# One plain tile pair instead of two in the second FFN, and the fourth block's low part by DMA

## The chip, the cores and the metric

The kernel runs on one core of a Trainium2 chip, in one launch. The metric is the time of one execution on the device, in microseconds (us); less is better. The kernel before takes 1185.99 us, the median of three executions from 1185.46 to 1186.32.

Five engines with queues of their own work side by side. TensorE (PE in the profile) multiplies matrices out of on-chip memory into accumulator banks, and loads stationary weights beside that (PEld). VectorE (DVE) and ScalarE (ACT) do elementwise work. GpSimd (POOL) issues the DMAs that add to what they write, and SyncE (SP) issues the ordinary loads.

## The reference

The program is one encoder layer and a final norm: FFN 1, a mixer of two recurrences, FFN 2. Two sequences of 256 tokens go through it. Of it the two FFNs matter here; both have a model width of 1024 and a hidden width of 2816:

```python
def swiglu(h, w_in, w_out):
    a, g = jnp.split(h @ w_in, [D_FF], axis=-1)
    return (jax.nn.silu(a) * g) @ w_out
...
    x = x + 0.5 * swiglu(rmsnorm(x, g_ffn1), w_ffn1_in, w_ffn1_out)
...
    x = x + 0.5 * swiglu(rmsnorm(x, g_ffn2), w_ffn2_in, w_ffn2_out)
```

Everything is float32.

## The kernel before

Both sequences are held together as 512 columns, with features on the 128 partitions, so `x` is eight tiles of 128 x 512. TensorE works in a rounded form of float32, so each operand is split: a high part (a cast to the rounded form) and a low part (value minus high part). A product takes three passes, high by high, high by low and low by high. So each weight tile must be split before it is used. There are two ways. `split2` casts on ScalarE (line 254) and subtracts on VectorE (line 255). `split_dma` casts on ScalarE, writes the negated value into the low tile on ScalarE too, and lets a GpSimd DMA add the weights to it from memory (lines 259 to 261); there VectorE has no part.

An FFN has 22 tile pairs, each a value tile and a gate tile of 128 features. They are computed in three ways:

- The first three pairs (`first_tiles`, tiles `f2i`) run before the norm of x is known, and are scaled by it later in `gated`.
- The next two are plain pairs (`w_plain`, `plain`, tiles `f2p`): 48 matmuls of 512 columns each, on split x. Their value tile's weights come through the tile kind `sum` and the pool `wb`, the gate tile's through `raw` and `wa`.
- The remaining 17 are seven-product units (tiles `f1s`, `f2s`). Value and gate tile by the two halves of the columns is a 2 x 2 block product, which is done with seven products instead of eight, on sums of the weights' four blocks and on sums of x. Each product is 12 matmuls of 256 columns, so a unit is 84.

The sums of x (`x_sums`, lines 310 to 313, tiles `xu`, `xv`, `xt`, `xw`, split into `xch` and `xcl`) are made once in an FFN. The weights of a unit come in two steps. `w_rows` loads them: blocks 1 and 2 into `raw[:, 0:2]`, block 3 into `sm[:, 0]`, block 4 into `raw[:, 2]` (SyncE, lines 335 to 337, "the third load" is that of line 337), and splits blocks 1 and 2 with the accumulating DMA (lines 339 to 341; `wah`, `wal`). `w_sums` forms the weight sums on VectorE (lines 347 to 350), splits three of them (`ah[:, 2:5]`), and then splits the sum in `raw[:, 1]` together with block 4 in `raw[:, 2]` (`wbh`, `wbl`, 1024 elements). Block 4 serves the seventh product, which runs only in the following unit.

`pair` is one unit. On TensorE come product y0 (block 1) and z1 (block 2), the sixth product of the unit before, y4, the seventh of the unit before, q2 and y3. Between them ScalarE copies banks: `m` after y0 (line 419), the right half of `u` after y4 (line 426), which must be done before y3 overwrites that bank, and the left half of `u` after y3 (line 432). VectorE's `t` (line 399) and ScalarE's silu (line 422) come from z1 and m.

The units are grouped in three parts of the hidden tiles (0 to 7, 8 to 14, 15 to 21), and each part is followed by eight output tiles. So the first part has three units, the others seven. `raw`, `sum`, `wa` and `wb` have two buffers each, so the loads of unit n+2 wait until unit n's splits have read theirs. The order of instructions on each engine is set by a scheduler when the program is built, and by a few explicit constraints (`tc.issue_after`); on the chip each queue then runs in that order and waits where its inputs aren't there.

Of the kernel before, what the change touches and what calls it, by code (L numbers as in the profile page):

```python
# [13 lines left out]
ALU = mybir.AluOpType  # L14
# [4 lines left out]
T = 512  # L19
# [17 lines left out]
def encoder_kernel(ctx: ExitStack, tc: tile.TileContext, xT, par, w2, gnorm, mask,  # L37
# [215 lines left out]
    def split2(hi, lo, src):  # L253
        rounded[:] = [nc.scalar.copy(hi, src).ins]
        return nc.vector.tensor_tensor(out=lo, in0=src, in1=hi.bitcast(F32), op=ALU.subtract)
# [76 lines left out]
    def w_rows(w_a, j, name):  # L332

        raw, sm = w_raw(name), w_sum(name)
        nc.sync.dma_start(raw[:, 0:2, :].rearrange("p a b -> p (a b)"), w_a[2 * j])
        nc.sync.dma_start(sm[:, 0, :], w_a[2 * j + 1][:, 0:T])
        nc.sync.dma_start(raw[:, 2, :], w_a[2 * j + 1][:, T:])
        (ah, al), (bh, bl) = w_pair("wa", 5, name), w_pair("wb", 2, name)
        nc.scalar.copy(ah[:, 0:2], raw[:, 0:2])
        nc.scalar.activation(al[:, 0:2], raw[:, 0:2], AF.Copy, scale=-1.0)  # L340
        nc.gpsimd.dma_start(al[:, 0:2].rearrange("p a b -> p (a b)"), w_a[2 * j], accum_op=ALU.add)
        return raw, sm, ah, al, bh, bl

    def w_sums(w_a, j, name, rows=None):

        raw, sm, ah, al, bh, bl = rows or w_rows(w_a, j, name)
        nc.vector.tensor_tensor(out=sm[:, 1], in0=sm[:, 0], in1=raw[:, 2], op=ALU.add)
        nc.vector.tensor_tensor(out=sm[:, 0::2], in0=sm[:, 0:2], in1=raw[:, 0:1].broadcast_to([P, 2, T]),
                                op=ALU.subtract)
        nc.vector.tensor_tensor(out=raw[:, 1], in0=raw[:, 1], in1=sm[:, 2], op=ALU.subtract)  # L350
        split2(ah[:, 2:5], al[:, 2:5], sm)
        split2(bh, bl, raw[:, 1:3])
        a, b = (lambda n: (ah[:, n], al[:, n])), (lambda n: (bh[:, n], bl[:, n]))

        return a(0), a(1), a(2), a(3), a(4), b(0), b(1)
# [37 lines left out]
        split2(hi, lo, raw)  # L393
        return hi, lo

    def ffn(w_a, w_o, xs_of, raws, dma_from, gcol, sq, name, done, last=None, squares={}, places=(None, None), rounds=None):

        L, R = slice(0, SEQ), slice(SEQ, T)
        add = lambda o, p, q: nc.vector.tensor_tensor(out=o, in0=p, in1=q, op=ALU.add)
        late, copied = [], []  # L400
        hs = []
        xc = []

        def finish(late, when):
            j, w, y, q, u, t, g = late
            if when == 0:
                product(y, w[5], xc[X22], False, True)
                nc.scalar.activation(t[:, R], y[:, :SEQ], AF.Silu)
            else:
                product(q, w[6], xc[XT4], False, True)  # L410
                add(g[:, L], q[:, :SEQ], u[:, R])
                hs.append(activate(t, g, f"{name}{j}"))

        def pair(j, w):
            y, z = acc(f"psy_{name}{j}"), acc(f"psz_{name}{j}")
            m, u = tmp(f"{name}m{j}"), tmp(f"{name}u{j}")
            t, g = tmp(f"{name}t{j}"), tmp(f"{name}g{j}")
            product(y, w[0], xc[X11], True, False)
            copied.append(nc.scalar.copy(m[:, L], y[:, :SEQ]).ins)
            product(z, w[1], xc[X21], True, True)  # L420
            add(t[:, L], z[:, :SEQ], m[:, L])
            nc.scalar.activation(t[:, L], t[:, L], AF.Silu)
            if late:
                finish(late[0], 0)
            product(y, w[4], xc[XT2], False, False)
            nc.scalar.copy(u[:, R], y[:, :SEQ])
            if late:
                finish(late.pop(), 1)
            q = acc(f"psq_{name}{j}", True)
            product(q, w[2], xc[XT3], True, False)  # L430
            product(y, w[3], xc[XT1], False, False)
            nc.scalar.copy(u[:, L], y[:, :SEQ])
            add(g[:, R], q[:, :SEQ], u[:, L])
            late.append((j, w, y, q, u, t, g))

        def out_tile(part, i, w):
            if late:
                finish(late[0], 0)
                finish(late.pop(), 1)
            hi, lo = w  # L440
            n = len(part)
            if last and part is parts[-1] and i == KD - 1:
                last(hi, lo, hs)
                return
            ps = acc(f"ps_{name}o{part[0]}_{i}", i % 2 == 0)
            for k in range(n):
                f = slice(k * P, (k + 1) * P)
                mm3(ps, hi[:, f], lo[:, f], *hs[k], k == 0, k == n - 1)
            nc.vector.scalar_tensor_tensor(out=x[i], in0=ps, scalar=0.5, in1=x[i], op0=ALU.mult, op1=ALU.add)  # L449
            if part is parts[-1]:  # L450
                done(i)
            if i == KD - 1:
                hs.clear()

        NP = NF // 2
        parts = [range(0, 8), range(8, 15), range(15, KF)]
        units = []
        for part in parts:
            for j in part:
                if j >= NP + 2:  # L460
                    units.append((lambda j=j: w_sums(w_a, j, f"{name}s{j}"), lambda w, j=j: pair(j, w)))
            for i in range(KD):
                units.append((lambda part=part, i=i: w_out_tile(w_o, part, i, f"{name}o{part[0]}_{i}"),
                              lambda w, part=part, i=i: out_tile(part, i, w)))

        pss, xs, marks = first_tiles(raws, xs_of, dma_from, f"{name}i", sq, squares)
        banks = [[acc(f"ps_{name}p{n}", True) for n in range(2)]]
        r, _ = rms_stat(sq, name, banks[0], [marks.get(m) for m in places])  # L470
        act_of = {}

        def gated(j, a, b):
            t, g = tmp(f"{name}t{j}"), tmp(f"{name}g{j}")
            nc.vector.tensor_tensor(out=t, in0=a, in1=r, op=ALU.mult)
            nc.scalar.activation(t, t, AF.Silu)
            nc.vector.tensor_tensor(out=g, in0=b, in1=r, op=ALU.mult)
            act_of[j] = t, g

        def act(j):  # L480
            act_of[j] = activate(*act_of[j], f"{name}{j}")

        def plain(pss, w):
            for ps, (hi, lo) in zip(pss, w):
                for k in range(KD):
                    f = slice(k * P, (k + 1) * P)
                    mm3(ps, hi[:, f], lo[:, f], *xs[k], k == 0, k == KD - 1)

        top = NP - 1
        steps = x_sums(gcol, r, name, marks)  # L490
        w_p = w_plain(w_a, NP, f"{name}p", (None, None) if rounds is None else (None,))
        for _ in range(4):
            next(steps)
        if rounds is not None:
            w_p += w_plain(w_a, NP, f"{name}p", (marks["x", rounds[0]],), 1)
        gated(top, pss[2 * top], pss[2 * top + 1])
        w_p2 = w_plain(w_a, NP + 1, f"{name}p2", (None, None) if rounds is None else [marks["x", n] for n in rounds])
        xc += next(steps)
        sums_done = x_last[0]
        plain(banks[0], w_p)  # L500
        gated(0, pss[0], pss[1])
        with tc.issue_after(sums_done):
            nxt = units[0][0]()
        banks.append([acc(f"ps_{name}p{n}", True) for n in range(2, 4)])
        plain(banks[1], w_p2)
        gated(1, pss[2], pss[3])
        for j in range(NP):
            act(j)
        for j in (NP, NP + 1):
            gated(j, *banks[j - NP])  # L510
            act(j)
        hs += [act_of[j] for j in range(NP + 2)]
        for n, (_, run) in enumerate(units):
            cur = nxt
            if n == 0:
                j = NP + 3
                rows = w_rows(w_a, j, f"{name}s{j}")
                run(cur)
                with tc.issue_after(copied[0]):
                    nxt = w_sums(w_a, j, f"{name}s{j}", rows)  # L520
            else:
                nxt = units[n + 1][0]() if n + 1 < len(units) else None
                run(cur)
# [10 lines left out]
    def sq_of(n):  # L534
# [1 line left out]
            sqs[n] = rp.tile([P, T], F32, tag="sq", name=f"sq{n}")  # L536
        return sqs[n]

    ffn(w_f1, w_o1, lambda k: split_x(k, C_G1, None, "a"), raw1, 4, C_G1, sq1, "f1", done1,
        squares={0: (0,), 1: range(1, 5), 2: range(5, KD)}, places=((2, 1), (3, 2)), rounds=(1, 2))  # L540
    sqm = sq_of("m")
    first_stage.close()
# [519 lines left out]
            scaled(0, rf[0], range(2, KD // 2))  # L1062
            scaled(1, rf[1], range(KD // 2))

    ffn(w_f2, w_o2, lambda k: xs2[k], raw2, 1, C_G2, sq_of("b"), "f2", done2, last2)
    last_stage.close()


# [86 lines left out]
```

## Time and profile before

| | |
|---|---|
| median of three executions | 1185.99 us |
| the profiled execution | 1186.56 us, span 1184.8 us |
| TensorE busy | 1171.2 us, 99% of the span, 6646 matmuls |
| VectorE busy | 729.9 us, 62% |
| ScalarE busy | 605.9 us, 51% |
| GpSimd busy | 112.4 us, 9% |
| granted TensorE clock | 0.996 of full speed, mean over the span |
| moved by DMA | 141.12 MB, 119 GB/s |

The span goes from the first to the last instruction of the profiled execution; the 1.76 us around it belong to the launch. A timeline row is one instruction: start and length in us, engine, line of the kernel, the tile written and the tiles read, and at the end in brackets how long the engine had been idle and what ended that. The chain of waits is followed back from the last instruction: each piece is the work, or the transfer, that the next one waited for.

### The profile page before, as it was taken

How to read it: one execution, taken by the hardware profiler on the slowest of the kernel's cores; microseconds unless marked ns; L12 is line 12 of the kernel's file. 1: busy time of each engine (PE TensorE's matmuls, PEld its weight loads, DVE VectorE, ACT ScalarE, POOL GpSimd, SP SyncE). 2: the span in 40 equal slices, each digit the busy share in tenths (PEclk: the TensorE clock that was granted, in tenths of full speed). 3: DMA queues.
4: the chain of work that ended last, by engine and by line, in shares of the span. 5: the costliest groups of instructions: out<-in, count | busy, mean ns of one | idle time of the engine just before them, and what ended most of it. 6: DMA issues, size and time to landing. Idle time of an engine off the chain costs nothing.

```text
span 1184.8 us, 16887 instructions
## 1 busy us (share of the span) xinstructions
PE 1171.2 (99%) x6646; PEld 1015.6 (86%) x6646; DVE 729.9 (62%) x1128; ACT 605.9 (51%) x990; POOL 112.4 (9%) x151
## 2 busy tenths in 40 slices
PE   9999999999999999999999999999999999999996
PEld 8898899899987888888888888888789899989985
DVE  7965576567547879557573453363685467566643
ACT  6763365356446665566663332254664256336642
POOL 2100000000021103030000000013100000000011
PEclk9999999999999999999999999999999999999998
DMA  9663455366414213232253323231864456445512
GB/s 263 146 165 116 116 138 143 112 141 163 124 54 129 91 55 116 74 105 76 76 187 116 93 95 116 66 112 30 203 145 132 118 126 154 130 122 147 155 47 72
DMA packets 58128, 141.12 MB, mean 119 GB/s; under 512 B 5568, under 2 KB 20128, under 8 KB 58048
## 3 DMA queue, kind: packets, MB, share of 16 engines
q1 hardware_dynamic: 47664, 110.44, 29.3%
q0 software_dynamic: 8176, 27.19, 13.3%
q10 hardware_dynamic: 2208, 2.41, 0.6%
q8 instruction: 52, 0.85, 0.3%
q14 instruction: 28, 0.23, 0.1%
HBM read 135.51 MB, written 2.11 MB: 116 GB/s over the span
## 4 chain that ended last, share of the span: by engine, by line
PE 88%; issue 4%; DMA 3%; DVE 3%; ACT 1%; POOL 0%; SPq 0%; DVEq 0%; ACTq 0%; POOLq 0%
PE psy_f L363 16%; PE psq_f L363 8%; PE psz_f L363 4%; PE ps_f1o L232 3%; PE ps_f1o L233 3%; PE ps_f1o L231 3%; PE ps_f2o L232 3%; PE ps_f2o L233 3%; PE ps_f2o L231 3%; PE ps_f2i L295 3%; PE pt_ga L619 3%; PE pt_ga L617 3%; PE pt_ga L618 3%; PE pt_gb L619 2%; PE pt_gb L617 2%
## 5 line engine op out<-in xcount | busy, mean ns | idle before, releaser
L363 PE MATMUL psy_f<-xch_f,wal_f2s 128*128 128x256 f32 x204 | 57.6, 282 | 0.4 <-DMA wal_f2s<-in_w_f 0.4
L363 PE MATMUL psy_f<-xch_f,wal_f1s 128*128 128x256 f32 x204 | 57.4, 281 | 0.4 <-DMA wal_f1s<-in_w_f 0.4
L363 PE MATMUL psy_f<-xch_f,wah_f2s 128*128 128x256 f32 x204 | 57.5, 282 | 0.0
L363 PE MATMUL psy_f<-xcl_f,wah_f1s 128*128 128x256 f32 x204 | 57.3, 281 | 0.0
L363 PE MATMUL psy_f<-xch_f,wah_f1s 128*128 128x256 f32 x204 | 57.3, 281 | 0.0
L363 PE MATMUL psy_f<-xcl_f,wah_f2s 128*128 128x256 f32 x204 | 57.1, 280 | 0.0
L619 PE MATMUL pt_ga<-whi_ga,xl_m 128*128 128x512 f32 x128 | 50.7, 396 | 0.0
L617 PE MATMUL pt_ga<-whi_ga,xh_m 128*128 128x512 f32 x128 | 50.7, 396 | 0.0
L619 PE MATMUL pt_gb<-whi_gb,xl_m 128*128 128x512 f32 x128 | 50.5, 396 | 0.0
L618 PE MATMUL pt_ga<-wlo_ga,xh_m 128*128 128x512 f32 x128 | 50.4, 394 | 0.0
L617 PE MATMUL pt_gb<-whi_gb,xh_m 128*128 128x512 f32 x128 | 50.4, 394 | 0.0
L618 PE MATMUL pt_gb<-wlo_gb,xh_m 128*128 128x512 f32 x128 | 50.4, 394 | 0.0
L94 DVE TENSOR_TENSOR wlo_ga<-raw_ga,whi_ga 128x1024 fp32r<-128x1024 f32 x16 | 19.6, 1224 | 46.4 <-ACT whi_ga L93 46.4
L449 DVE SCALAR_TENSOR_TENSOR x<-ps_f2o,x 128x512 f32<-128x512 f32 x23 | 15.8, 689 | 41.6 <-PE ps_f2o L233 41.6
L93 ACT CAST whi_gb<-raw_gb 128x1024 fp32r<-128x1024 f32 x16 | 16.8, 1048 | 45.7 <-PE pt_ga L619 28.8
L94 DVE TENSOR_TENSOR wlo_gb<-raw_gb,whi_gb 128x1024 fp32r<-128x1024 f32 x16 | 19.6, 1224 | 32.7 <-ACT whi_gb L93 32.7
L449 DVE SCALAR_TENSOR_TENSOR x<-ps_f1o,x 128x512 f32<-128x512 f32 x24 | 16.5, 689 | 36.6 <-PE ps_f1o L233 36.6
L363 PEld LDWEIGHTS psy_f<-xch_f,wal_f2s 128*128 128x128 f32 x204 | 38.5, 189 | 0.6 <-DMA wal_f2s<-in_w_f 0.6
L363 PEld LDWEIGHTS psy_f<-xch_f,wal_f1s 128*128 128x128 f32 x204 | 38.5, 189 | 0.6 <-DMA wal_f1s<-in_w_f 0.6
L363 PEld LDWEIGHTS psy_f<-xcl_f,wah_f2s 128*128 128x128 f32 x204 | 38.5, 189 | 0.1
L363 PEld LDWEIGHTS psy_f<-xch_f,wah_f1s 128*128 128x128 f32 x204 | 38.5, 189 | 0.1
L363 PEld LDWEIGHTS psy_f<-xch_f,wah_f2s 128*128 128x128 f32 x204 | 38.4, 188 | 0.2
(1163 smaller groups left out, 4037.2 us busy)
## 6 DMA issues: line engine op xcount, KB each, us to landing
raw_f1s<-in_w_f SPq DMA_DIRECT2D x17, 512.0 KB, 3.6
wal_f1s<-in_w_f POOLq DMA_DIRECT2D x17, 512.0 KB, 5.6
raw_f2s<-in_w_f SPq DMA_DIRECT2D x17, 512.0 KB, 3.6
wal_f2s<-in_w_f POOLq DMA_DIRECT2D x17, 512.0 KB, 5.6
raw_ga<-in_w_tm SPq DMA_DIRECT2D x16, 512.0 KB, 3.6
raw_gb<-in_w_tm SPq DMA_DIRECT2D x16, 512.0 KB, 3.5
sum_f1s<-in_w_f SPq DMA_DIRECT2D x17, 256.0 KB, 3.3
raw_f1s<-in_w_f SPq DMA_DIRECT2D x17, 256.0 KB, 3.9
```

The lines of the kernel that those rows point to most:

```text
L93: nc.scalar.copy(hi[:, :width], raw[:, :width])
L94: nc.vector.tensor_tensor(out=lo[:, :width], in0=raw[:, :width], in1=hi.bitcast(F32)[:, :width], op=ALU.subtract)
L231: nc.tensor.matmul(ps, lhsT=wh, rhs=xh, start=start, stop=False)
L232: nc.tensor.matmul(ps, lhsT=wh, rhs=xl, start=False, stop=False)
L233: nc.tensor.matmul(ps, lhsT=wl, rhs=xh, start=False, stop=stop)
L295: marks[k, n] = nc.tensor.matmul(pss[m], lhsT=w[:, f[m]], rhs=xp, start=k == n == 0, stop=k == KD - 1 and n == 2).ins
L363: nc.tensor.matmul(ps, lhsT=l[:, f], rhs=m, start=start and k == n == 0, stop=stop and k == 3 and n == 2, skip_group_check=True)
L449: nc.vector.scalar_tensor_tensor(out=x[i], in0=ps, scalar=0.5, in1=x[i], op0=ALU.mult, op1=ALU.add)
L617: nc.tensor.matmul(pss[t], lhsT=xh, rhs=hi[:, ws], start=k == 0, stop=False)
L618: nc.tensor.matmul(pss[t], lhsT=xh, rhs=lo[:, ws], start=False, stop=False)
L619: nc.tensor.matmul(pss[t], lhsT=xl, rhs=hi[:, ws], start=False, stop=k == KD - 1)
```

## The change

`ffn` gets a parameter `extra`, the number of plain pairs. FFN 1 keeps two, FFN 2 has one, so there 18 pairs are seven-product units, four of them in the first part. With one plain pair, `gated` of the third first pair and of the others is written at other places, and the second pair of accumulator banks isn't taken. In all units of both FFNs (35), the split of block 4 moves to `w_rows`: two ScalarE instructions of 512 elements and an accumulating DMA of 256 KB on GpSimd. `w_sums` then splits 512 elements there instead of 1024. Line numbers below the first edit rise by three.

```diff
--- before.py
+++ after.py
@@ -339,6 +339,9 @@
         nc.scalar.copy(ah[:, 0:2], raw[:, 0:2])
         nc.scalar.activation(al[:, 0:2], raw[:, 0:2], AF.Copy, scale=-1.0)
         nc.gpsimd.dma_start(al[:, 0:2].rearrange("p a b -> p (a b)"), w_a[2 * j], accum_op=ALU.add)
+        nc.scalar.copy(bh[:, 1], raw[:, 2])
+        nc.scalar.activation(bl[:, 1], raw[:, 2], AF.Copy, scale=-1.0)
+        nc.gpsimd.dma_start(bl[:, 1], w_a[2 * j + 1][:, T:], accum_op=ALU.add)
         return raw, sm, ah, al, bh, bl
 
     def w_sums(w_a, j, name, rows=None):
@@ -349,7 +352,7 @@
                                 op=ALU.subtract)
         nc.vector.tensor_tensor(out=raw[:, 1], in0=raw[:, 1], in1=sm[:, 2], op=ALU.subtract)
         split2(ah[:, 2:5], al[:, 2:5], sm)
-        split2(bh, bl, raw[:, 1:3])
+        split2(bh[:, 0], bl[:, 0], raw[:, 1])
         a, b = (lambda n: (ah[:, n], al[:, n])), (lambda n: (bh[:, n], bl[:, n]))
 
         return a(0), a(1), a(2), a(3), a(4), b(0), b(1)
@@ -393,7 +396,7 @@
         split2(hi, lo, raw)
         return hi, lo
 
-    def ffn(w_a, w_o, xs_of, raws, dma_from, gcol, sq, name, done, last=None, squares={}, places=(None, None), rounds=None):
+    def ffn(w_a, w_o, xs_of, raws, dma_from, gcol, sq, name, done, extra, last=None, squares={}, places=(None, None), rounds=None):
 
         L, R = slice(0, SEQ), slice(SEQ, T)
         add = lambda o, p, q: nc.vector.tensor_tensor(out=o, in0=p, in1=q, op=ALU.add)
@@ -457,7 +460,7 @@
         units = []
         for part in parts:
             for j in part:
-                if j >= NP + 2:
+                if j >= NP + extra:
                     units.append((lambda j=j: w_sums(w_a, j, f"{name}s{j}"), lambda w, j=j: pair(j, w)))
             for i in range(KD):
                 units.append((lambda part=part, i=i: w_out_tile(w_o, part, i, f"{name}o{part[0]}_{i}"),
@@ -493,27 +496,34 @@
             next(steps)
         if rounds is not None:
             w_p += w_plain(w_a, NP, f"{name}p", (marks["x", rounds[0]],), 1)
-        gated(top, pss[2 * top], pss[2 * top + 1])
-        w_p2 = w_plain(w_a, NP + 1, f"{name}p2", (None, None) if rounds is None else [marks["x", n] for n in rounds])
+        if extra > 1:
+            gated(top, pss[2 * top], pss[2 * top + 1])
+            w_p2 = w_plain(w_a, NP + 1, f"{name}p2", (None, None) if rounds is None else [marks["x", n] for n in rounds])
         xc += next(steps)
         sums_done = x_last[0]
+        if extra == 1:
+            gated(top, pss[2 * top], pss[2 * top + 1])
         plain(banks[0], w_p)
-        gated(0, pss[0], pss[1])
+        if extra > 1:
+            gated(0, pss[0], pss[1])
         with tc.issue_after(sums_done):
             nxt = units[0][0]()
-        banks.append([acc(f"ps_{name}p{n}", True) for n in range(2, 4)])
-        plain(banks[1], w_p2)
+        if extra > 1:
+            banks.append([acc(f"ps_{name}p{n}", True) for n in range(2, 4)])
+            plain(banks[1], w_p2)
+        else:
+            gated(0, pss[0], pss[1])
         gated(1, pss[2], pss[3])
         for j in range(NP):
             act(j)
-        for j in (NP, NP + 1):
+        for j in range(NP, NP + extra):
             gated(j, *banks[j - NP])
             act(j)
-        hs += [act_of[j] for j in range(NP + 2)]
+        hs += [act_of[j] for j in range(NP + extra)]
         for n, (_, run) in enumerate(units):
             cur = nxt
             if n == 0:
-                j = NP + 3
+                j = NP + extra + 1
                 rows = w_rows(w_a, j, f"{name}s{j}")
                 run(cur)
                 with tc.issue_after(copied[0]):
@@ -536,7 +546,7 @@
             sqs[n] = rp.tile([P, T], F32, tag="sq", name=f"sq{n}")
         return sqs[n]
 
-    ffn(w_f1, w_o1, lambda k: split_x(k, C_G1, None, "a"), raw1, 4, C_G1, sq1, "f1", done1,
+    ffn(w_f1, w_o1, lambda k: split_x(k, C_G1, None, "a"), raw1, 4, C_G1, sq1, "f1", done1, 2,
         squares={0: (0,), 1: range(1, 5), 2: range(5, KD)}, places=((2, 1), (3, 2)), rounds=(1, 2))
     sqm = sq_of("m")
     first_stage.close()
@@ -1062,7 +1072,7 @@
             scaled(0, rf[0], range(2, KD // 2))
             scaled(1, rf[1], range(KD // 2))
 
-    ffn(w_f2, w_o2, lambda k: xs2[k], raw2, 1, C_G2, sq_of("b"), "f2", done2, last2)
+    ffn(w_f2, w_o2, lambda k: xs2[k], raw2, 1, C_G2, sq_of("b"), "f2", done2, 1, last2)
     last_stage.close()
```

Three places of the instruction queues follow, before and after. Names end in a running number of the tile, which differs between the two programs.

VectorE at the end of the first tiles of FFN 2, before: the last sums of x, where `f2t` and `f2g` are the third first pair.

```order
L255 TENSOR_TENSOR xcl_f_7775<-xw_f_7755,xch_f_7774 128x512
L475 TENSOR_TENSOR f2t_7778<-ps_f2i_7485,r_f_7686 128x512
L477 TENSOR_TENSOR f2g_7779<-ps_f2i_7486,r_f_7686 128x512
L310 SCALAR_TENSOR_TENSOR xu_f_7797<-x_81,pt,r_f_7686 128x512
L310 SCALAR_TENSOR_TENSOR xv_f_7798<-x_85,pt,r_f_7686 128x512
L313 TENSOR_TENSOR xt_f_7799<-xu_f_7797 128x256
```

After:

```order
L255 TENSOR_TENSOR xcl_f_7846<-xt_f_7831,xch_f_7845 128x512
L255 TENSOR_TENSOR xcl_f_7850<-xw_f_7832,xch_f_7849 128x512
L350 TENSOR_TENSOR sum_f2s_7907<-sum_f2s_7907,raw_f2s_7906 128x512
L351 TENSOR_TENSOR sum_f2s_7907<-sum_f2s_7907,raw_f2s_7906 128x2x512
L478 TENSOR_TENSOR f2t_7853<-ps_f2i_7536,r_f_7737 128x512
L480 TENSOR_TENSOR f2g_7854<-ps_f2i_7537,r_f_7737 128x512
```

The last sums of x (`xu`, `xv`, `xt`, `xw`) now stand ahead of the first pair's multiplies, and so do the two sums of unit 0 (`sum_f2s`).

ScalarE in unit 0 of FFN 2, from the copy `m` to the copy `u`, before; `wah` and `wbh` belong to unit 1, `f24hh` to the last plain pair.

```order
L419 COPY f2m_7997<-psy_f_7995 128x256
L254 CAST wah_f2s_7988<-sum_f2s_7984 128x1536
L254 CAST f24hh<-f2t_7973 128x512
L422 ACTIVATE f2t_7999<-f2t_7999 128x256
L254 CAST wbh_f2s_7990<-raw_f2s_7983 128x1024
L426 COPY f2u_7998<-psy_f_7995 128x256
```

After:

```order
L422 COPY f2m_7980<-psy_f_7978 128x256
L254 CAST wah_f2s_7968<-sum_f2s_7964 128x1536
L254 CAST f23hh<-f2t_7953 128x512
L425 ACTIVATE f2t_7982<-f2t_7982 128x256
L254 CAST wbh_f2s_7970<-raw_f2s_7963 128x512
L429 COPY f2u_7981<-psy_f_7978 128x256
```

The order is the same, with half as long a cast of `wbh`; the other half stands further ahead in the queue.

VectorE in a unit in the middle of FFN 1, before, from the split of unit n's weight sums (`wal`) to its last split (`wbl`); `sum_f1s_2750` belongs to unit n+1.

```order
L255 TENSOR_TENSOR wal_f1s_2632<-sum_f1s_2627,wah_f1s_2631 128x1536
L399 TENSOR_TENSOR f1t_2649<-psz_f_2646,f1m_2647 128x256
L347 TENSOR_TENSOR sum_f1s_2750<-sum_f1s_2750,raw_f1s_2749 128x512
L348 TENSOR_TENSOR sum_f1s_2750<-sum_f1s_2750,raw_f1s_2749 128x2x512
L399 TENSOR_TENSOR f1g_2527<-psq_f_2599,f1u_2525 128x256
L368 TENSOR_TENSOR f1t_2526<-f1g_2527,f1t_2526 128x512
L255 TENSOR_TENSOR wbl_f1s_2634<-raw_f1s_2626,wbh_f1s_2633 128x1024
```

After; here `sum_f1s_2792` is that of unit n+1.

```order
L350 TENSOR_TENSOR sum_f1s_2792<-sum_f1s_2792,raw_f1s_2791 128x512
L255 TENSOR_TENSOR wal_f1s_2671<-sum_f1s_2666,wah_f1s_2670 128x1536
L402 TENSOR_TENSOR f1t_2691<-psz_f_2688,f1m_2689 128x256
L351 TENSOR_TENSOR sum_f1s_2792<-sum_f1s_2792,raw_f1s_2791 128x2x512
L402 TENSOR_TENSOR f1g_2566<-psq_f_2638,f1u_2564 128x256
L371 TENSOR_TENSOR f1t_2565<-f1g_2566,f1t_2565 128x512
L255 TENSOR_TENSOR wbl_f1s_2673<-raw_f1s_2665,wbh_f1s_2672 128x512
```

The first sum of unit n+1 (line 347 before, 350 after), which needs its third load, moved from behind `t` to ahead of `wal`, and the last split has 512 elements instead of 1024.

## Rows read from the trace of the kernel before

**Rows 1.** The page's first part: busy us (share of the span) x instructions.

```profile
PE 1171.2 (99%) x6646; PEld 1015.6 (86%) x6646; DVE 729.9 (62%) x1128; ACT 605.9 (51%) x990; POOL 112.4 (9%) x151
```

**Rows 2.** Windows, second plain pair of FFN 2 (start:end length; busy us by engine; clock).

```profile
866.97:878.12 11.15, 11.15 (x49) 9.03 (x48) 9.23 (x12) 7.15 (x10) 0.86 (x1) 1.00 0.58 142
```

**Rows 3.** Chain of waits, second FFN: start us, us, what.

```profile
880.39 5.73 DMA wal_f2s<-in_w_f
...
959.40 2.84 PE psy_f L363 x24
...
969.35 2.84 PE psy_f L363 x24
```

**Rows 4.** Chain of waits, first FFN.

```profile
263.54 2.83 PE psy_f L363 x24
...
273.44 2.83 PE psy_f L363 x24
```

**Rows 5.** TensorE's waits by line: us in total, times, longest.

```profile
PE psy_f L363 <- DMA wal_f1s<-in_w_f: 0.4, 1, 0.4
```

**Rows 6.** Timeline, TensorE at unit 0's end, FFN 2: start, us, line, idle before.

```profile
883.84 0.39 PE L363 MATMUL psy_f<-xch_f,wah_f2s 128*128 128x256 f32 x1
...
885.47 0.28 PE L363 MATMUL psy_f<-xcl_f,wah_f2s 128*128 128x256 f32 x1
886.16 0.39 PE L363 MATMUL psy_f<-xch_f,wal_f2s 128*128 128x256 f32 x1 [0.41 <-DMA wal_f2s<-in_w_f]
```

**Rows 7.** Timeline, ScalarE at FFN 2's gated tiles and unit 0.

```profile
855.33 0.63 ACT L476 ACTIVATE f2t<-f2t 128x512 f32<-128x512 f32 x1
...
882.15 0.42 ACT L422 ACTIVATE f2t<-f2t 128x256 f32<-128x256 f32 x1
882.47 1.05 ACT L254 CAST wbh_f2s<-raw_f2s 128x1024 fp32r<-128x1024 f32 x1
883.41 0.37 ACT L426 COPY f2u<-psy_f 128x256 f32<-128x256 f32 x1
```

**Rows 8.** Timeline, VectorE before and in unit 0, FFN 2.

```profile
872.02 1.22 DVE L255 TENSOR_TENSOR wbl_f2s<-raw_f2s,wbh_f2s 128x1024 fp32r<-128x1024 f32 x1
...
878.09 0.69 DVE L347 TENSOR_TENSOR sum_f2s<-sum_f2s,raw_f2s 128x512 f32<-128x512 f32 x1 [1.19 <-DMA raw_f2s<-in_w_f]
...
881.63 0.42 DVE L399 TENSOR_TENSOR f2t<-psz_f,f2m 128x256 f32<-128x256 f32 x1
```

**Rows 9.** DMA issues: tile, queue, count, KB each, median us to landing.

```profile
raw_f1s<-in_w_f SPq DMA_DIRECT2D x17, 256.0 KB, 3.9
...
wal_f1p<-in_w_f POOLq DMA_DIRECT2D x2, 512.0 KB, 8.5
...
wal_f2p<-in_w_f POOLq DMA_DIRECT2D x2, 512.0 KB, 7.3
```

**Rows 10.** Timeline, SyncE's loads: FFN 2's unit 2, FFN 1's long stretch.

```profile
873.65 0.53 SPq L337 DMA_DIRECT2D raw_f2s<-in_w_f  x1
...
274.80 0.33 SPq L335 DMA_DIRECT2D raw_f1s<-in_w_f  x1
275.18 0.43 SPq L337 DMA_DIRECT2D raw_f1s<-in_w_f  x1
```

**Rows 11.** DMA queue of GpSimd: packets, MB, share of 16 engines.

```profile
q0 software_dynamic: 8176, 27.19, 13.3%
```

**Rows 12.** Timeline, VectorE in a middle unit of FFN 1.

```profile
268.55 1.76 DVE L255 TENSOR_TENSOR wal_f1s<-sum_f1s,wah_f1s 128x1536 fp32r<-128x1536 f32 x1 [0.68 <-ACT wah_f1s L254]
...
273.55 1.22 DVE L255 TENSOR_TENSOR wbl_f1s<-raw_f1s,wbh_f1s 128x1024 fp32r<-128x1024 f32 x1
```

**Rows 13.** Timeline, ScalarE in the same unit.

```profile
271.95 1.05 ACT L254 CAST wbh_f1s<-raw_f1s 128x1024 fp32r<-128x1024 f32 x1 [0.60 <-PE psq_f L363]
...
274.78 1.05 ACT L339 CAST wah_f1s<-raw_f1s 128x1024 fp32r<-128x1024 f32 x1 [0.49 <-PE psy_f L363]
```

**Rows 14.** Timeline, GpSimd in the same stretch.

```profile
277.35 0.86 POOL L341 DMA_DIRECT2D wal_f1s<-in_w_f  x1 [9.04 <-ACT wal_f1s L340]
```

## The prediction

> **What bounds the kernel now.** I read the page's first part, then windows over the stage that changes, then the chain of waits, then the queues of the waiting engines. TensorE is busy 99% of the span, VectorE 62% and ScalarE 51% [rows 1], so only work taken off TensorE, or waits put on it, can move the end. In the second FFN the second plain pair runs from 866.97 to 878.12 with TensorE busy all 11.15 us [rows 2]. After it come the seven-product units; in the chain one unit begins at 959.40 and the next at 969.35, TensorE all the way: 9.95 us each [rows 3]. In the first FFN the step is 263.54 to 273.44, 9.90 us [rows 4]. TensorE waits, or nearly does, at two places that the change touches. The first is unit 1's first weights, once in each FFN, where it stands for the low part that the accumulating DMA brings (the first FFN's in [rows 5]). In the second FFN this DMA is issued at 880.39 and takes 5.73 us [rows 3]; the first product of unit 1 that needs it runs at 886.16 instead of 885.59 (9.95 / 84 is 0.118 for a matmul, and 885.47 was the one before): 0.57 us lost, of which the row shows 0.41 [rows 6]. A second place is just in time: product y3 of unit 0 starts at 883.84 [rows 6], when ScalarE's copy u of the bank before it is done (883.41 + 0.37) [rows 7].
>
> **Part 1: one plain pair less, one unit more, in the second FFN.** 11.15 goes and 9.95 comes: -1.20 us. Nothing else runs on TensorE for it, so all of it is on the path.
>
> What becomes late instead is looked for at the head of the units. Call T the end of the plain work: 878.12 before, 866.97 after. Three things must be there.
>
> (a) Unit 0's own low weights. The new order puts the last sums of x and unit 0's first two sums ahead of the gated tile's first multiply. The sums of x fall into time in which VectorE was idle; the two others are 0.7 and 1.1 us more in front (0.69 for 512 elements [rows 8], twice the elements less the fixed part for the other), so ScalarE's silu goes from 855.33 [rows 7] to about 857.1, the low cast (1.05) follows at 857.7, and the DMA goes out at about 859.1. With the 5.73 of the units' kind [rows 3] it lands at 864.8, with the 7.3 of the plain pairs' at 866.4, with the first FFN's 8.5 at 867.6 [rows 9]; needed at T + 0.24 = 867.2. From 2.4 early to 0.4 late: I take no wait, since 7.3 is this stage's own.
>
> (b) Unit 0's copy u, before product y3. On ScalarE it stands behind silu and a cast in both orders. In the old one silu began at 882.15, the cast of 1024 at 882.47, u at 883.41 [rows 7]. Silu waits for VectorE's t (881.63 to 882.05), and t stands behind the first sum of unit 2 at 878.09, which waited 1.19 us for unit 2's third load [rows 8]; that load was issued at 873.65 [rows 10], so 4.4 us. So t starts 3.54 us after that sum, wherever the sum is. In the new order the load is freed when unit 0's last split ends. That was 872.02 + 1.22 [rows 8]; in the new order it is about 863.4 (from 857.7, 0.95 + 0.95 + 1.4 for ScalarE's casts of 1024, 1024 and 1536 at the rate of [rows 7], then 1.76 [rows 12] and 0.69 for the two splits), and the load goes out at about 863.9, T - 3.07 instead of T - 4.47. It lands at T + 1.33 (T - 0.07 before), so t is 1.39 late against T. The cast between silu and u is half as long (0.53 of the two starts' 0.94), which gives 0.43 back: u and y3 0.96 later. The new accumulating DMA of unit 1 goes out at nearly the same time as that load; bounds for what it takes from it: nothing, or 1.5 us, the packet time of 256 KB on its queue (13.3% of 1184.8 us for 27.19 MB, 5.8 us per MB) [rows 11]. So y3 is 0.96 to 2.5 late; I take 1.1, near the lower end, as transfers share and need not queue.
>
> (c) Unit 1's low weights. Cast and issue follow T as before and the landing at T + 8.0 too. With y3 0.96 later or more the first product that needs them is at 885.59 + 0.96, T + 8.43, or later: the 0.57 wait is gone, covered by (b).
>
> Net of (b) and (c): 1.1 - 0.57 = +0.5, with bounds -0.57 (both go) and +1.9.
>
> **Part 2: the fourth block by DMA, in all 35 units.** Per unit VectorE splits 512 instead of 1024 (1.22 to 0.69: -0.53) [rows 12, 8]. ScalarE does three casts of 512 for one of 1024; from one start to the next it is 0.94 for the 1.05 of 1024 [rows 7], so for the 0.63 of 512 about 0.52: +0.6. In a unit of the middle ScalarE idles 0.60 ahead of this cast and 0.49 ahead of the next unit's first [rows 13], 1.09 in these two gaps alone, so 0.6 has room; and u now stands ahead of silu, so no bank is copied later. Cost zero; without that cover it would be 0.1 us at most per unit on copy m, 3.5 in all. GpSimd issues 35 DMAs of 0.86 us more, an engine that waits 9.04 us between issues [rows 14].
>
> The new DMA itself has until the end of the following unit, over 10 us. What it can delay is the next unit's own low part: issued 277.35 [rows 14], it lands 5.73 later at 283.08 if it takes what unit 1's took [rows 3]. Its unit starts at 273.44 + 9.90 + 1.42 = 284.76 (of the chain's 24 products the first 12 are the unit's before [rows 4]), and needs it 0.24 behind that: slack 1.92 us. Zero. The first FFN's head keeps its order of casts on TensorE's side, so its wait [rows 5] stays: zero.
>
> The products of the new unit run at the same pace, but the units' pace differs by 0.04 between the FFNs without a row that says why; on 35 units that is 1.4 us either way, which I keep for the range.
>
> **Sum.** -1.20 + 0.5 = -0.7. The profiled execution was 1186.56 with a span of 1184.8, 0.57 above the median of 1185.99; on the median: **1185.3 us**.
>
> **Rivals.**
> A. The full saving: unit 2's third load lands as early as before, only the 0.57 wait stays. For it: the load's length of 4.4 was itself over the usual 3.9 [rows 9]. Against it: its release is 1.4 us later by the order. 1185.99 - 1.20 = 1184.8; with the 0.57 waits of both FFNs gone as well, 1183.6.
>
> B. Unit 0's low weights late, as the 8.5 landing [rows 9] would have it: 0.4 us of wait at T, and all of (b) moves with it, +0.4 on the forecast: 1185.7. At 12 us, a time no row shows, it would be +4.
>
> C, slower: a loop through VectorE. In the long stretches the new order puts the next unit's first sum, which waits for the third load, ahead of the split of this unit's sums. So a ring closes: third load, first sum, ..., last split, which frees the buffer for the next third load. Its length: from the split's start 268.55 to the last split's 273.55 5.00, in which the sum also lay before [rows 12]; the last split 0.69; 0.03 to the next issue and 0.38 between the two issues [rows 10]; landing 3.9 [rows 9]: 10.0 us, against a pace of 9.90. On that sum it drifts 0.1 per unit, three rings in each of the four seven-unit stretches, nothing against 0.53 (the shorter split's head start) plus 1.92 of slack. But the new DMA goes out about 1.2 us ahead of these loads (271.95 + 0.52 + 0.63 = 273.1 by the casts [rows 13]; 274.80 - 0.53 [rows 10]). If it holds them up by its whole 1.5 us, a ring drifts 1.6, three 4.8, less 2.45: 2.35 us per stretch, four stretches, +9.4: 1194.7. It decides from 0.82 a ring, a landing of 4.6 instead of 3.9. For it: the DMAs of this kind that ran among other loads took 8.5 [rows 9] against 5.73. Against: the queues' share of the 16 engines is 13.3% on GpSimd's [rows 11], there is room, and two transfers that overlap in part share.
> The Trainium skill's "DMA: Bandwidth & Descriptors", section "Issuing engines are not separate DMA queues", says that DMAs from scalar, sync and gpsimd end on the same 16 DMA engines and interleave. By that rule GpSimd's new transfers do slow SP's loads, which speaks for C, and for the upper part of (b); the rows of the crowded landings agree with it.
>
> D. ScalarE's copies come late after all, by up to 0.1 us in each of the 35 units, as its 0.6 us more per unit allow: up to +3.5, 1188.8. Against it: the gaps of [rows 13].
>
> **How the numbers follow.** Forecast 0.50, A 0.18 (0.06 of it the double gain that reaches 1183.6), B 0.12, C 0.12, D 0.08. What a measurement can tell from no change is 0.2%, 2.4 us: faster is below 1183.6, slower above 1188.4. Faster gets the 0.06; slower C and a quarter of D (its end above the bound): 0.14; the rest is same, 0.80. The range takes the double gain (1183.6), and above it B, the upper end of (b) at 1186.7 and the pace's 1.4 on top: 1188.2.
>
> **What would show it.** One plain pair of 11.15 in the second FFN's stage, ended about 11.15 earlier; y3 of unit 0 starting 6.7 to 6.9 after T instead of 5.72, behind ScalarE's u; no TensorE wait for the second FFN's low weights of unit 1, the same wait in the first FFN; steps of 9.90 and 9.95 in the chain. Wrong: a TensorE wait for low weights in the middle of a seven-unit stretch (C), steps above 9.95 with TensorE behind ScalarE's copies (D), or a wait at T (B).

## The result: 1200.25 us, slower

The changed kernel takes 1200.25 us (median of four, 1200.05 to 1200.52), the kernel before 1185.93 beside it: 1.012 times as long, interval 1.0108 to 1.0131. The forecast of 1185.3 was wrong, and so was its range. Most of the loss, 10.8 of the 13.5 us that the profiled executions differ by, is that of rival C, a ring through VectorE, to which the prediction gave 0.12; the rest is lost at the head of FFN 2.

The first part of the page after, which answers to [rows 1]:

```profile
PE 1175.1 (98%) x6682; PEld 1019.2 (85%) x6682; DVE 715.5 (60%) x1134; ACT 625.0 (52%) x1064; POOL 142.5 (12%) x185
```

VectorE is busy 14 us less and ScalarE 19 us more, as the edits would have it; TensorE is busy 4 us longer, though a unit is shorter than a plain pair. Where TensorE waits is in its list of waits (line waited at, what for: us in total, times, longest), which answers to [rows 5]:

```profile
PE psy_f L366 <- ACT f2m L422: 4.5, 5, 1.8
PE psy_f L366 <- ACT f1m L422: 3.3, 6, 0.8
...
PE psy_f L366 <- DMA wal_f2s<-in_w_f: 1.1, 1, 1.1
...
PE psy_f L366 <- DMA wal_f1s<-in_w_f: 0.9, 1, 0.9
...
PE psy_f L366 <- ACT f2u L429: 0.7, 1, 0.7
```

Before, these products waited twice, 0.4 us each. Now they wait 14 times, 10.5 us in all, and most of it (7.8 us) for `m`, ScalarE's copy of the bank after y0, which the prediction had late by 0.1 us a unit at most, and that from ScalarE's own work.

Windows put the loss in its places. Each row is one stretch of the program on TensorE: start and end, length, then the busy time of TensorE, its weight loads, VectorE, ScalarE and GpSimd, granted clock, share of the DMA engines, GB/s. The kernel before, in this order: second and third stretch of FFN 1 (seven units each), FFN 2 from the first plain pair to the end of its first units, second and third stretch of FFN 2:

```profile
139.18:210.16 70.98, 70.98 (x596) 70.58 (x595) 45.67 (x60) 41.44 (x66) 4.32 (x5) 1.00 0.58 145
247.79:318.77 70.98, 70.98 (x596) 70.58 (x595) 46.78 (x61) 41.43 (x66) 4.32 (x5) 1.00 0.59 146
855.82:910.48 54.66, 54.25 (x356) 49.18 (x355) 39.73 (x57) 31.62 (x49) 3.46 (x4) 1.00 0.59 150
953.55:1024.79 71.24, 71.24 (x596) 70.83 (x595) 45.73 (x60) 41.46 (x66) 4.32 (x5) 1.00 0.56 144
1062.39:1133.63 71.24, 71.24 (x596) 70.83 (x595) 47.10 (x62) 41.47 (x66) 4.32 (x5) 1.00 0.57 145
```

The same five after:

```profile
139.95:213.63 73.68, 71.76 (x596) 70.75 (x595) 43.69 (x61) 44.30 (x78) 9.53 (x11) 1.00 0.67 161
251.25:324.41 73.16, 71.74 (x596) 70.74 (x595) 44.94 (x62) 44.10 (x78) 9.53 (x11) 1.00 0.70 163
860.76:918.18 57.42, 54.84 (x392) 51.65 (x391) 38.22 (x54) 36.35 (x58) 6.08 (x7) 0.97 0.63 151
961.28:1034.60 73.32, 72.02 (x596) 71.00 (x595) 43.47 (x61) 44.35 (x78) 9.53 (x11) 1.00 0.68 161
1072.22:1147.28 75.06, 72.44 (x596) 71.13 (x595) 44.66 (x62) 44.15 (x78) 9.53 (x11) 1.00 0.66 159
```

The four stretches of seven units lose 2.70, 2.18, 2.08 and 3.82 us, 10.8 together, and the head of FFN 2, which should have gained, loses 2.76. That is 13.5, all that the profiled executions differ by (1198.3 against 1184.8 of span).

**The ring.** The chain of waits in the third stretch of FFN 1, after (start, length, what; the short pieces between are left out):

```profile
284.06 0.09 DVE sum_f1s L350
...
284.67 1.75 DVE wal_f1s L255
286.42 0.34 DVE f1t L402
286.76 1.13 DVE sum_f1s L351
287.89 0.35 DVE f1g L402
...
288.94 0.70 DVE wbl_f1s L255
...
289.65 0.33 SPq L335
...
290.03 4.76 DMA raw_f1s<-in_w_f
...
295.43 1.75 DVE wal_f1s L255
```

This is rival C's ring, step for step: the next unit's first sum, the split of the sums, t, the next unit's second sum, g, the last split, which frees the buffer; the next loads go out at 289.65 and 290.03; the third load lands 4.76 later, and only then come the following first sum and, behind it, the next split. One turn takes 295.43 - 284.67 = 10.76 us (the one before it 10.52), and TensorE's unit 9.90 [rows 4]. From the first sum to the next third load it is 290.03 - 284.06 = 5.97 us; the prediction had 6.1 for this part, so what made the turn long is the landing. What makes TensorE feel it is the queue on ScalarE. Its rows in the same unit, after:

```profile
289.06 0.62 ACT L254 CAST f117hh<-f1t 128x512 fp32r<-128x512 f32 x1 [0.29 <-DVE f1t L371]
289.58 1.05 ACT L339 CAST wah_f1s<-raw_f1s 128x1024 fp32r<-128x1024 f32 x1
...
291.76 1.47 ACT L254 CAST wah_f1s<-sum_f1s 128x1536 fp32r<-128x1536 f32 x1
293.12 0.36 ACT L422 COPY f1m<-psy_f 128x256 f32<-128x256 f32 x1
```

The first of them waits for VectorE (0.29 idle), and behind it stand three weight casts and then the copy m, whose 0.36 end at 293.48. TensorE's y4 starts at once when it has it:

```profile
293.54 0.39 PE L366 MATMUL psy_f<-xch_f,wah_f1s 128*128 128x256 f32 x1 [0.36 <-ACT f1m L422]
```

Before, m came at this time of a unit, on ScalarE and then TensorE:

```profile
268.42 0.36 ACT L419 COPY f1m<-psy_f 128x256 f32<-128x256 f32 x1
```

```profile
269.02 0.28 PE L363 MATMUL psy_f<-xch_f,wah_f1s 128*128 128x256 f32 x1
```

It ended at 268.78, and y4 started at 269.02: there were at most 0.24 us to spare, not the 1.92 that the prediction had found for the low weights. By the starts of TensorE's matmuls these waits are the whole loss of that stretch: y4 starts 0.76, 0.64 and 0.86 us behind the matmul before it in three units, and the matmul behind it 0.22 later each time, where a step is otherwise 0.118; that makes 2.2, and the stretch lost 2.18.

The median landing of the third load, in FFN 1 (which answers to the first of [rows 9]) and in FFN 2; before, it was 3.9 in both:

```profile
raw_f1s<-in_w_f SPq DMA_DIRECT2D x17, 256.0 KB, 4.8
...
raw_f2s<-in_w_f SPq DMA_DIRECT2D x18, 256.0 KB, 5.0
```

**The head of FFN 2.** VectorE's two first sums of units 1 and 2, after, which answer to the second of [rows 8]:

```profile
863.59 0.69 DVE L350 TENSOR_TENSOR sum_f2s<-sum_f2s,raw_f2s 128x512 f32<-128x512 f32 x1 [2.12 <-DMA raw_f2s<-in_w_f]
...
876.85 0.69 DVE L350 TENSOR_TENSOR sum_f2s<-sum_f2s,raw_f2s 128x512 f32<-128x512 f32 x1 [1.84 <-DMA raw_f2s<-in_w_f]
```

Unit 1's first sum now stands right behind the third first pair's multiplies, ahead of those of the two other first pairs (before it stood behind them all), and waited 2.12 us for its load; all the other gated tiles wait behind it. Unit 2's waited 1.84. The chain of waits joins the two (pieces between are left out):

```profile
856.01 7.46 DMA raw_f2s<-in_w_f
...
870.12 0.70 DVE wbl_f2s L255
...
871.21 5.62 DMA raw_f2s<-in_w_f
...
880.48 0.35 DVE f2t L402
```

Unit 1's third load took 7.46 us to land. From the sum that waited for it VectorE is in the chain up to unit 0's last split at 870.12; that frees the buffer of unit 2's third load, which went out at 871.21 and landed 5.62 later; its sum held up t, and t held up silu and u. So ScalarE came to its copies m and u late, in the row for m because silu and two casts stood ahead of it:

```profile
876.34 0.35 ACT L422 COPY f2m<-psy_f 128x256 f32<-128x256 f32 x1
...
881.68 0.36 ACT L429 COPY f2u<-psy_f 128x256 f32<-128x256 f32 x1
```

and TensorE waited for both:

```profile
876.75 0.49 PE L366 MATMUL psy_f<-xch_f,wah_f2s 128*128 128x256 f32 x1 [1.84 <-ACT f2m L422]
877.03 0.42 PE L366 MATMUL psy_f<-xcl_f,wah_f2s 128*128 128x256 f32 x1
...
882.10 0.39 PE L366 MATMUL psy_f<-xch_f,wah_f2s 128*128 128x256 f32 x1 [0.74 <-ACT f2u L429]
```

T, the end of the plain pair, was 871.91 here. y4 began 4.84 us behind it, where two products of 1.42 would have it at 2.84; y3 began 10.19 behind it, where the kernel before had 5.72 and the prediction 6.7 to 6.9. The second row shows something else: after the wait a matmul of 256 columns takes 0.42 and not 0.28. The windows of the two products before the wait and of the 3.6 us after it (the clock is the third figure from the right):

```profile
871.91:874.90 2.99, 2.99 (x25) 2.79 (x23) 2.99 (x6) 2.40 (x5) 0.00 (x0) 1.00 0.96 240
876.70:880.30 3.60, 3.55 (x17) 3.56 (x18) 3.45 (x5) 1.75 (x2) 0.87 (x1) 0.53 0.56 73
```

The granted clock fell from 1.00 to 0.53, its lower level of 1.2 GHz but for the last moment; 16 matmuls at 0.213 instead of 0.118 are 1.5 us more. So q2, which follows y4, ended 3.5 late, 2.0 from y4's start and the rest from slower matmuls. But these 3.5 are not added to the head's loss: even so TensorE stood idle for 0.74 us before y3 could start, and the chain of waits comes to y3 through unit 2's load, t and u, not through y4. What the head lost is y3's 10.19 instead of 5.72, 4.47 us, less the 1.20 that the new unit saves and the 0.57 of the wait that is gone: 2.70, and 2.76 was measured.

### The profile page after: what moved, and what is told of

It is laid out like the page before. It is cut to its first block, busy times and chain, and to the rows that moved or that the text cites. A ratio compares the mean times of both kernels' runs of the same rounds, so it can differ in the third digit from the quotient of the medians.

```text
span 1198.3 us, 17169 instructions
## 1 busy us (share of the span) xinstructions
PE 1175.1 (98%) x6682; PEld 1019.2 (85%) x6682; DVE 715.5 (60%) x1134; ACT 625.0 (52%) x1064; POOL 142.5 (12%) x185
## 4 chain that ended last, share of the span: by engine, by line
PE 74%; DVE 9%; DMA 8%; issue 4%; ACT 4%; POOL 0%; SPq 0%; DVEq 0%; ACTq 0%; POOLq 0%
PE psy_f L366 8%; DMA raw_f2s<-in_w_f 4%; PE psq_f L366 4%; PE ps_f1o L232 3%; PE ps_f1o L233 3%; PE ps_f1o L231 3%; PE ps_f2o L232 3%; PE ps_f2o L231 3%; PE ps_f2o L233 3%; PE pt_ga L629 2%; PE pt_ga L627 2%; PE pt_ga L628 2%; PE pt_gb L629 2%; PE pt_gb L627 2%; PE pt_gb L628 2%
## 5 line engine op out<-in xcount | busy, mean ns | idle before, releaser
L366 PE MATMUL psy_f<-xch_f,wah_f2s 128*128 128x256 f32 x216 | 62.2, 288 | 5.4 <-ACT f2m L422 4.5
L366 PE MATMUL psy_f<-xch_f,wal_f2s 128*128 128x256 f32 x216 | 61.5, 285 | 1.1 <-DMA wal_f2s<-in_w_f 1.1
L366 PE MATMUL psy_f<-xcl_f,wah_f2s 128*128 128x256 f32 x216 | 61.0, 283 | 0.0
L366 PEld LDWEIGHTS psy_f<-xch_f,wah_f2s 128*128 128x128 f32 x216 | 41.0, 190 | 7.2 <-ACT f2m L422 5.9
L366 PEld LDWEIGHTS psy_f<-xch_f,wal_f2s 128*128 128x128 f32 x216 | 41.3, 191 | 1.3 <-DMA wal_f2s<-in_w_f 1.3
L366 PEld LDWEIGHTS psy_f<-xcl_f,wah_f2s 128*128 128x128 f32 x216 | 41.3, 191 | 0.1
L350 DVE TENSOR_TENSOR sum_f2s<-sum_f2s,raw_f2s 128x512 f32<-128x512 f32 x18 | 12.5, 692 | 46.2 <-DMA raw_f2s<-in_w_f 34.7
```

The costliest lines, as they stand in the source:

```text
L366: nc.tensor.matmul(ps, lhsT=l[:, f], rhs=m, start=start and k == n == 0, stop=stop and k == 3 and n == 2, skip_group_check=True)
```

## The experiments

All times below are TensorE's, from the first matmul of a stretch to the end of its last, in the one profiled execution of each run; the last column is the median of all executions, with the ratio to the kernel before and its interval.

| run | FFN 1, 2nd | FFN 1, 3rd | FFN 2, head | FFN 2, 2nd | FFN 2, 3rd | median us, ratio |
|---|---|---|---|---|---|---|
| before | 70.98 | 70.98 | 54.66 | 71.24 | 71.24 | 1185.65 to 1185.93 |
| after | 73.68 | 73.16 | 57.42 | 73.32 | 75.06 | 1200.25, 1.0120 (1.0108 to 1.0131) |
| one plain pair alone | 70.98 | 70.98 | 57.79 | 71.24 | 71.24 | 1188.77, 1.0023 (1.0013 to 1.0033) |
| DMA alone | 73.31 | 74.02 | 54.43 | 73.20 | 73.15 | 1194.90, 1.0079 (1.0063 to 1.0095) |
| order back in the long stretches | 70.98 | 70.98 | 58.03 | 71.24 | 71.24 | 1189.92, 1.0036 (1.0023 to 1.0048) |
| small DMA | 71.20 | 71.00 | 56.79 | 71.24 | 71.45 | 1187.79, 1.0019 (1.0010 to 1.0029) |
| order back in the heads | 74.63 | 73.83 | 53.19 | 74.46 | 73.50 | 1196.16, 1.0085 (1.0071 to 1.0099) |
| order back everywhere | 71.13 | 70.99 | 53.87 | 71.24 | 71.25 | 1184.86, 0.9989 (0.9980 to 0.9998) |
| one plain pair, order back | 70.98 | 70.99 | 54.04 | 71.24 | 71.25 | 1184.65, 0.9991 (0.9982 to 1.0000) |

**One plain pair alone.** The changed kernel without the second edit:

```diff
-        nc.scalar.copy(bh[:, 1], raw[:, 2])
-        nc.scalar.activation(bl[:, 1], raw[:, 2], AF.Copy, scale=-1.0)
-        nc.gpsimd.dma_start(bl[:, 1], w_a[2 * j + 1][:, T:], accum_op=ALU.add)
...
-        split2(bh[:, 0], bl[:, 0], raw[:, 1])
+        split2(bh, bl, raw[:, 1:3])
```

> Only the first part of the change: one plain pair in FFN 2, block 4 split as before (1024 elements on ScalarE and VectorE, no new DMA). Ring theory (the 10.8 us lost in the four seven-unit stretches come from VectorE's wait for the third load, which the new order puts ahead of the sums' split): all four stretches back at 66.7 and 66.9 us; what is left is -1.2 for the pair and the head of FFN 2, whose order is nearly that of the changed kernel: 1185 to 1188. Rival (TensorE is slowed by what the new instructions take from ScalarE and the DMA engines, whatever VectorE's order): nothing of it is here either, 1184.8.

1188.77, just above what was expected. The long stretches are as before; but in them the scheduler has also put the first sum back behind t, so this run does not part the order from the transfer there. The head keeps the early sum and loses as much as in the changed kernel, so the head's loss is not the new DMA's. Its rows: VectorE's first sum of unit 1, and TensorE's third matmul of unit 0, the first that reads the low weights.

```profile
858.64 0.69 DVE L347 TENSOR_TENSOR sum_f2s<-sum_f2s,raw_f2s 128x512 f32<-128x512 f32 x1 [3.47 <-DMA raw_f2s<-in_w_f]
```

```profile
870.04 0.36 PE L363 MATMUL psy_f<-xch_f,wal_f2s 128*128 128x256 f32 x1 [2.58 <-DMA wal_f2s<-in_w_f]
```

The sum held VectorE for 3.47 us, silu and the low cast of unit 0 came late, and here it was unit 0's own low weights that TensorE waited for, at T as in rival B, but because their cast came late.

**DMA alone.** Two plain pairs in FFN 2 (`extra` 2), the second edit in all units.

```diff
-    ffn(w_f2, w_o2, lambda k: xs2[k], raw2, 1, C_G2, sq_of("b"), "f2", done2, 1, last2)
+    ffn(w_f2, w_o2, lambda k: xs2[k], raw2, 1, C_G2, sq_of("b"), "f2", done2, 2, last2)
```

> Only the second part: block 4's low part by DMA in all units, two plain pairs in both FFNs. Ring theory: the four seven-unit stretches keep their loss of 2.1 to 3.8 us each, the head of FFN 2 does not: 1186 + 10.8 + 0.5 = 1197. If the loss came from the moved gated tiles and the missing pair instead, 1186.

The four stretches lose 2.33, 3.04, 1.96 and 1.91, 9.2 together, and the head nothing; the total is 2 us below what was expected. The two parts of the change are slower each by itself (3.1 and 9.2 us against the kernel before beside them), and the sum is 12.4 of the 14.3. Most of what lacks shows in the last stretch, 3.8 with both parts and 1.9 here, but single stretches differ by about 1 us between these runs.

**Order back in the long stretches.** Nothing is removed; the first sum of a unit, in tiles 8 and up, is queued behind t of the unit that runs.

```diff
-        nc.vector.tensor_tensor(out=sm[:, 1], in0=sm[:, 0], in1=raw[:, 2], op=ALU.add)
+        with at(behind.get("g" if rows else "t") if j >= 8 else None):
+            nc.vector.tensor_tensor(out=sm[:, 1], in0=sm[:, 0], in1=raw[:, 2], op=ALU.add)
...
-            add(t[:, L], z[:, :SEQ], m[:, L])
+            behind["t"] = add(t[:, L], z[:, :SEQ], m[:, L]).ins
```

> The changed kernel with one edge more: in tiles 8 and up the first sum of a unit (the instruction that waits for the third load) is queued on VectorE behind t of the unit that runs, as before the change; all DMAs and ScalarE's work stay. Ring theory: the loss of the four long stretches goes, 10.8 us: 1189.5, with their lengths at 66.7 to 67.2. Rival (DMA and ScalarE work as such): no change, 1200.

1189.92, as the ring has it: 10.3 us come back by one edge in VectorE's queue. First a long stretch, then the head:

```profile
138.84:209.82 70.98, 70.98 (x596) 70.58 (x595) 44.98 (x62) 45.01 (x78) 9.53 (x11) 1.00 0.69 167
855.43:913.46 58.03, 54.52 (x392) 51.48 (x391) 38.19 (x54) 36.45 (x58) 6.08 (x7) 0.97 0.63 152
```

In the stretch TensorE is busy all 70.98 us, with all of the DMAs and with ScalarE's 45.0 us of work, so neither costs anything by itself. The loads still take 5.0 us at the median. A first sum of the long stretch, the next third load (of the same unit as above), and the sum that reads it:

```profile
280.13 0.68 DVE L352 TENSOR_TENSOR sum_f1s<-sum_f1s,raw_f1s 128x512 f32<-128x512 f32 x1
```

```profile
284.31 0.46 SPq L338 DMA_DIRECT2D raw_f1s<-in_w_f  x1
```

```profile
290.03 0.68 DVE L352 TENSOR_TENSOR sum_f1s<-sum_f1s,raw_f1s 128x512 f32<-128x512 f32 x1
```

It is read 5.72 us after its issue, and nothing waits. The ring is still there, but the long split stands outside of it now: from a first sum to the next third load it takes 4.18 us instead of 5.97, with a landing of 5.1 (the median in FFN 1) 9.3 in all, less than the 9.90 of TensorE's unit.

**Small DMA.** The order of the changed kernel, with a sixteenth of the new transfer; the kernel leaves out the adding of block 4's weights to its low part in 120 of the 128 partitions.

```diff
-        nc.gpsimd.dma_start(bl[:, 1], w_a[2 * j + 1][:, T:], accum_op=ALU.add)
+        nc.gpsimd.dma_start(bl[0:8, 1], w_a[2 * j + 1][0:8, T:], accum_op=ALU.add)
```

> The changed kernel, where the new accumulating DMA carries only 8 of its 128 partitions (16 KB instead of 256 KB), so the low part of block 4 is left wrong in the other 120; order of all instructions as in the changed kernel. If the ring needs the slow landing (third load 5.0 us beside the new transfer, 3.9 without): ring 10.0 us instead of 10.5 to 11.0, the long stretches within 0.5 us of before, total 1190 to 1191. If the order alone or ScalarE's three casts make the loss: 1198 to 1200.

The other half of the ring: its order is there, but the third load lands in 4.1 us instead of 5.0,

```profile
raw_f2s<-in_w_f SPq DMA_DIRECT2D x18, 256.0 KB, 4.1
```

and the long stretches lose 0.22, 0.02, 0.00 and 0.21. So in the long stretches order and transfer are both needed, and either alone costs nearly nothing. The total came out 2 us below what was expected, since that allowed 0.5 us of loss to each stretch and kept the head at its old loss, of which 0.6 went.

**Order back in the heads.** The same edge in tiles below 8 only, and at unit 1 (`rows` given) the anchor is the second first pair's last multiply.

```diff
-            nc.vector.tensor_tensor(out=g, in0=b, in1=r, op=ALU.mult)
+            ins = nc.vector.tensor_tensor(out=g, in0=b, in1=r, op=ALU.mult).ins
+            if j == 1:
+                behind["g"] = ins
```

> The changed kernel with the queueing edit only in tiles below 8 (the heads and first stretches); the long stretches keep the changed kernel's order. Theory: they keep 2.1 to 3.8 us of loss each, 10.8 in all, and the head loses nothing: 1185 + 10.8 = 1195 to 1196.5. Rival (the head's lateness is what starts the drift of the later stretches): well below that, 1190.

The head takes 53.19, 1.47 less than before the change, and the four stretches lose 3.65, 2.85, 3.22 and 2.26, 12.0 together; 1196.16 is inside what was expected. A late head is not what starts the ring. The edge moves two sums of the head at once, unit 1's behind the first pairs' multiplies and unit 2's behind t, so what each is worth rests on the chain of waits alone.

**Order back everywhere.** Both edges, without the condition on `j`.

> The changed kernel with every unit's first sum queued on VectorE behind t of the unit that runs, and at the head of each FFN unit 1's first sum behind the gated tiles' multiplies; nothing else. Theory: both losses are waits of VectorE for a third load that stands too far ahead in its queue, so both go: four stretches at 66.7 and 66.9 us, the first stretch of FFN 2 (four units) from 42.5 to 37.3 to 38.3: 1184.3 to 1185.6. Rival (the head has too little time after one plain pair, whatever the order: unit 0's and 1's splits don't fit into 11.15 us): the head stays at 41 or more, 1189 to 1190.

1184.86, inside what was expected and 1.07 us (0.1%) under the kernel before, interval 0.2 to 2.4. Stretch and head, and the one wait of TensorE that is left in the head:

```profile
139.12:210.25 71.13, 71.13 (x596) 70.66 (x595) 44.91 (x62) 44.86 (x78) 9.50 (x11) 1.00 0.67 167
855.14:909.01 53.87, 53.19 (x392) 50.14 (x391) 38.65 (x54) 36.28 (x58) 6.06 (x7) 1.00 0.68 167
```

```profile
872.66 0.39 PE L368 MATMUL psy_f<-xch_f,wah_f2s 128*128 128x256 f32 x1 [0.53 <-ACT f2u L431]
```

**One plain pair, order back.** The first run of these with the same edges, so without the new DMA.

> One plain pair in FFN 2, block 4 split as before without the new DMA, and every unit's first sum queued behind t, unit 1's behind the gated tiles. Theory: as in the run with all DMAs and this order, the first stretch of FFN 2 at 37.3 to 38.3 instead of 42.2, and the others as before: 1184.3 to 1185.6, so the new DMA buys nothing where nothing waits for VectorE. If the DMA is worth something in itself, this is slower than that run by 0.5 us or more.

1184.65, not to be told from the run with the DMA. The new DMA is worth nothing measurable here, where nothing in the long stretches waits for VectorE.

## Why the prediction was wrong, by its steps

Two steps failed: the zero of part 2, which measured 10.8 us, and the 1.1 of (b), which measured 4.47.

- **Part 1, -1.20.** Right as far as the runs show it: the plain pair that is left takes 11.15, and with the order back the head takes 53.87, 53.19 and 54.04 in three runs, 0.79, 1.47 and 0.62 less than before.
- **(a), unit 0's low weights.** The step took no wait at T, and in the changed kernel there is none. But it did not see unit 1's first sum, which follows right behind the gated tile's two multiplies in the queue. With one plain pair alone that sum stands ahead of them, and there the wait at T came, 2.58 us.
- **(b), copy u before y3.** This is the step that failed in the head. The mechanism was right: unit 2's first sum waited for its load, 1.84 us, and y3 came behind u. What was wrong is when that load goes out. The prediction worked out the end of unit 0's last split from ScalarE's casts and had the load at T - 3.07; it went out at 871.21, T - 0.70, mostly because VectorE had stood 2.12 us at unit 1's first sum. And it took 5.62 us instead of 4.4, inside the bound of 1.5 more that the prediction gave. Together y3 was 4.47 late, where 1.1 was taken and 2.5 was the upper bound. With the order back unit 2's first sum stands behind t, so this wait cannot arise; u is late by 0.53 in the row even so. There VectorE works without a wait from 859.61 until t at 870.96, which is T + 4.68 (before, T + 3.51), so it is its work and not a load that holds t.
- **(c), unit 1's low weights.** Right: that wait is gone, covered by u.
- **Part 2, cost zero.** Wrong, and for the reason that stands in rival C. ScalarE's 0.6 us a unit are free (all of it is there in the 70.98 us). What failed is the sentence on what the new DMA can delay: it looked at unit n+1's low weights, with 1.92 us of slack, and at no load of SyncE's. The third load went from 3.9 to 4.8 us in FFN 1 and 5.0 in FFN 2.
- **Rival C.** The mechanism and the place were right, and the price came near (9.4 us against 10.8); the weight of 0.12 was too low. It decided from a landing of 4.6, and the argument against it, that two transfers share when they overlap in part, gave no number. With the ring at 10.0 us against 9.90 even at 3.9, there was no room at all, and only the slack behind it spoke for zero. That slack was wrong as well: 0.24 at m instead of 1.92, because the ring pushes ScalarE's casts, and m stands behind them. So the near price is in part luck: a delay of 0.9 to 1.1 instead of 1.5 and a slack too large are two wrong sizes that met.
- **D, ScalarE's copies late by 0.1 a unit.** m is late, but by the ring, not by ScalarE's own work.

The Trainium skill's "DMA: Bandwidth & Descriptors", section "Issuing engines are not separate DMA queues", says that DMAs started by the scalar, sync or gpsimd engine run on the same 16 DMA engines and interleave. The runs agree in so far as SyncE's load in FFN 2 takes 5.0 us with GpSimd's 256 KB ahead of it and 4.1 with 16 KB. In the prediction the rule spoke for C, and C came.

What stays open: the last stretch loses 3.82 in the changed kernel, and the others 2.1 to 2.7. In that stretch TensorE also waited once for low weights (1.1 us, the third line of the waits); by the starts of its matmuls that place takes 1.4 us, and the other 2.4 are like the other stretches. Why those weights came late there is not shown. With the same order and transfers in the long stretches, the run with the order back in the heads loses 2.26 in that stretch, without such a wait.

## What to carry to other kernels

Before an engine's shorter work is booked as free, follow the new order of its queue, and for each instruction that reads a load ask when that load lands: one that waits holds all behind it. Where a load, its reader and the release of its buffer close a ring, add up the ring and set it against the pace of the bound engine; at 10.0 against 9.9 it is already lost when something lengthens the landing. And ask of a transfer moved onto the DMA queues which loads beside it will land later (here by 0.9 to 1.1 us); the cheaper cure may be one edge in the order.

## What was not expected of the hardware

A wait can cost TensorE more than its length, and the length alone does not tell. After 1.84 us of waiting in the changed kernel its granted clock was at 0.53 for 3.6 us, as shown above; there the slower matmuls were hidden, since TensorE had to wait for u behind them. After the 2.58 us with one plain pair alone, the first five matmuls still ran at full speed, and the clock was 0.50 from 872 to 874 us; no wait for u or m followed, so the 1.4 us that 15 slow matmuls took more were not hidden. But a wait of 2.36 us for m, with the small DMA, left the clock at 1.00 in the 3.43 us behind it, and so did one of 1.14 us, in the changed kernel's last stretch:

```profile
1100.70:1104.00 3.30, 3.26 (x27) 3.26 (x28) 2.13 (x4) 3.30 (x5) 0.56 (x2) 1.00 0.80 161
```

What decides between the two is not shown here.
